# A matmul with a decayed running sum: a quarter of w loaded in eight pieces, the first 32 slots replanned, the last blocks copied in two pieces and stored by two queues

## The chip, the cores and the metric

The kernel runs on one core of a Trainium2 chip. The metric is the device time of one execution in microseconds (us). The kernel before takes 905.96 us, the median of three runs (905.82 to 906.7). The profile belongs to one execution; its span, from the first to the last instruction, is 903.9 us.

## The reference

`x` has shape (16, 2048, 1024), `w` (1024, 1024), `decay` (1024,), all float32. For every batch the product is taken and then summed along time with a decay that each column has for itself:

```python
xw = x @ w
out[:, 0, :] = xw[:, 0, :]
for t in range(1, S):
    out[:, t, :] = decay[None, :] * out[:, t - 1, :] + xw[:, t, :]
```

## The kernel before

**The layout.** Time is cut into 64 chunks of 512 steps (`TL`), two chunks make a group. The 1024 output columns are eight sets `n` of 128 (`K = 8`; the sets 0 to 3 are the first half `h = 0` of the columns, 4 to 7 the second, `R = 4`), and the 1024 input columns are eight sets `k`. TensorE forms 128 columns x 512 or 1024 steps in PSUM with `wsb[:, k, n]` as the weights and a transposed chunk of x, and VectorE runs the scan along time. A pair of a group and a set `n` is a slot. 

**x comes in** through GpSimd's DMA queue, four transfers for a chunk (the quads `q`), converted to bf16 on the way. VectorE transposes it (`T`, or `E` in quarters of a half chunk), and ScalarE or VectorE puts it in order for TensorE (`X`, `Y`, or `F`, `G`). For some products TensorE reads the transposed chunk `xw` directly.

```python
    def load(c, q, j0=0, j1=NJ):
        b, t0 = chunks[c]
        if c not in xb_of:
            xb_of[c] = ring(sb, "xb", 3, [128, NJ, CQ], BF16)
        pin(nc.gpsimd.dma_start(
            out=xb_of[c][quad(q), j0:j1],
            in_=_ap(x, [[D, P], [P * D, j1 - j0], [1, CQ]],
                    (b * S + t0 + j0 * P) * D + q * CQ)))
```

**w comes in** in four quarters: `(h, e)` is the half of the output columns and the parity of `k`. Quarter (0, 0) comes as float32 through the queues of SyncE (SP) and ScalarE (ACT), the other three through GpSimd's, as bf16. `settle` copies one set of 128 rows, `k = 2 m + e`, to its place in `wsb`; it reads all four quads of the staging tile.

```python
    def load_w(queues, h, e):
        for i, q in enumerate((0, 2, 1, 3)):
            pin(queues[i % len(queues)].dma_start(
                out=stage[h, e][quad(q)].rearrange("p (m d) -> p m d", m=M),
                in_=_ap(w, [[2 * D, P], [2 * P * D, M], [1, CH]],
                        (q * CQ + e) * D + h * CH)))

    def settle(h, e, m, copy):
        src = stage[h, e][:, m * CH:(m + 1) * CH]
        pin(copy(out=wcols[:, 2 * m + e, h],
                 in_=src.rearrange("p (q r i) -> p q r i", q=NQ, r=R)))

```

In the plan `U0`, `U1`, `U2` are the quarters (0, 1), (1, 0), (1, 1), and `W` or `w` with a number i is `settle(i // 8, i // 4 % 2, i % 4)` on VectorE or on ScalarE: 0 to 3 settle the first quarter, 4 to 7 the second, 8 to 11 the third, 12 to 15 the fourth. `M0` to `M3` are the half chunks of the first two chunks of x.

**The order of the products at the start**, in which all even k of the first chunk come first, then the odd k, then the second chunk:

```python
        if step == 0:
            heads = [ring(psp, "ps", 3, [128, T]) for _ in range(3)]
            firsts = [ps[:, 0:TL] for ps in heads] + [spares[0]]
            seconds = [ps[:, TL:T] for ps in heads] + [spares[1]]
            for j0, j1 in halves:
                for k in range(0, K, 2):
                    for i in range(R):
                        matmul(firsts[i], i, k, xt_of[0], j0 * P, j1 * P, pairs=xw_of[0])
            for k in range(1, K, 2):
                for i in range(R):
                    matmul(firsts[i], i, k, xt_of[0])
            for k0 in range(0, K, 2):
                for i in range(R):
                    for k in (k0, k0 + 1):
                        matmul(seconds[i], i, k, xt_of[1], 0, H * P,
                               pairs=xw_of[1] if k0 < 4 else None)
            for i in range(R):
                for k in range(K):
                    matmul(seconds[i], i, k, xt_of[1], H * P, TL, H * P,
                           pairs=xw_of[1] if i < 2 else None)
```

**A slot is finished in one of two ways.** An unpaired tile is scanned by VectorE straight from PSUM. A paired one is halved first: ScalarE copies it out (`p`) and scales its odd steps (`g`), GpSimd adds neighbours (`j`), VectorE scans half the steps (`S`), ScalarE (`h`) and GpSimd (`c`) fill in the other half. `flips` names the slots that are turned from one way to the other. `B` is VectorE's transpose of the result into an output tile `ot`; when four of them are there, four stores of 32 rows each go out, and the tile's buffer is one of four.

```python
        def scan(self):
            T, n, so = self.T, self.n, self.so
            if self.paired:
                pin(nc.vector.tensor_tensor_scan(
                    out=so[:, 3:T + 2:2],
                    data0=squares[-1][:, n:n + 1].to_broadcast([128, T // 2]),
                    data1=self.xs[:, 1:T:2],
                    initial=0.0 if self.prev is None else self.prev,
                    op0=ALU.mult,
                    op1=ALU.add,
                ))
            else:
                parts = self.ps if isinstance(self.ps, tuple) else (self.ps,)
                size = T // len(parts)
                for i, ps in enumerate(parts):
                    self.run(ps, i * size, size)

    ...

        def store(self, b, t0):
            n0 = self.ns[0]
            c0 = n0 % R * P
            size = len(self.ns) * P
            for i, q in enumerate((0, 2, 1, 3)):
                pin(self.queues[i % len(self.queues)].dma_start(
                    out=_ap(out, [[D, P], [P * D, self.nj], [1, size]],
                            (b * S + t0 + self.t0) * D + n0 // R * CH + q * CR + c0),
                    in_=self.ot[quad(q), :, c0:c0 + size]))
```

**The plan** says for each slot what is recorded after its products; a capital or small letter is a deed of the kind above, `L` is one transfer of x, `k` keeps the last column for the next group. The first lines, slot -99 being what stands before all products:

```python
-99: "M0 M1 U0 M2 M3 U1 U2 w0 W1 w2 W3 K0 K1 K2 K3 E0 E1 G0 E2 G1 E3 F2 G3 E4 E5 G4 E6 G5 E7 F6 G7 W4 w5 W6 W7 D E8 E9 G8 E10 G9 E11 F10 G11 E12 L E13 G12 L E14 G13 E15 L F14 G15",
0: "p0 z0 W8 W9 W10 W11",
1: "g0",
2: "L S1 L",
3: "p2 z2 L g2 j0 S3 w12 w13 L w14 L w15 k1",
4: "j2 B1 d k3",
5: "p4 L S0 L g4 S2 L k0 h0 j4 B3 h2",
6: "k2 c0 T2 c2 p5 g5 B0 L X2 L",
7: "B2 L L Y2 T3 L z4 z5 j5 p6 S4 z6 L g6 L X3 S5 j6 S7 Y3 L S6 h4 k7 k5 c4 k4 h5 B7",
    ...
flips = (1, 13, 15, -19, -18, -16, -11, -8, -6, -3, -2)
```

**The end.** The last chunk's second half of columns isn't transposed by VectorE but by TensorE, against an identity, in four blocks of 128 steps; each block is copied out of PSUM and stored:

```python
    def ending(i):
        b, t0 = chunks[-1]
        nb = TL // 128
        pts = [ring(psp, name, count, [128, R, 128])
               for name, count in (("spare1", 1), ("ps", 3), ("ps", 3), ("spare", 1))]
        wides = [ring(sb, *spot, [128, NQ, R, P])
                 for spot in (("xb", 3), ("xb", 3), ("xb", 3), ("h", 4))]

        def cross(blocks, rs):
            for i in blocks:
                for r in rs:
                    t = 2 + i * 128
                    pin(nc.tensor.transpose(
                        out=pts[i][:, r], in_=tiles[r - R].so[:, t:t + 128], identity=ident))

        def leave(i, copy):
            pin(copy(out=wides[i].rearrange("p q r i -> p r q i"),
                     in_=pts[i].rearrange("p r (q i) -> p r q i", q=NQ)))
            pin(nc.sync.dma_start(
                out=_ap(out, [[D, 128], [1, CH]], (b * S + t0 + i * 128) * D + CH),
                in_=wides[i].rearrange("p q r i -> p (q r i)")))

        cross((0,), range(R))
        cross((1,), range(R))
        cross((2, 3), range(R - 1))
        cross((2, 3), (R - 1,))
        for i in range(nb):
            leave(i, (nc.scalar.copy, nc.vector.tensor_copy)[i % 2])
```

Every transfer has a semaphore to count to when it lands. GpSimd's transfers share eight of them in turn, those of SP and ACT another eight; a transfer waits until the one that had the semaphore before it has landed. The queue, the engine and the semaphore's place in the turn come from the framework's scheduler, not from the lines above.

Of the kernel before, what the change touches and what calls it, by code (L numbers as in the profile page):

```python
# [14 lines left out]
def _ap(ap_obj: bass.AP, new_ap, extra_offset=0):  # L15
    return dataclasses.replace(
        ap_obj,
        ap=[list(p) for p in new_ap],
        offset=ap_obj.offset + extra_offset,
    )  # L20
# [5 lines left out]
def kernel(  # L26
# [26 lines left out]
    nc = tc.nc  # L53
    pin = tc.keep_in_program_order
    B, S, D = x.shape
    assert w.shape == (D, D)

    NQ = 4
    P = 32
    CQ = D // NQ  # L60
    K = CQ // P
    M = K // 2
# [3 lines left out]
    R = K // 2  # L66
    CH = D // 2
# [8 lines left out]
    def ring(pool, name, count, shape, dtype=FP32):  # L76
        i = turns[name] = turns.get(name, -1) + 1
        return pool.tile(shape, dtype, name=f"{name}{i % count}")

    def quad(q):  # L80
        return slice(q * P, (q + 1) * P)
# [59 lines left out]
    class Tile:  # L141
# [39 lines left out]
        def copy(self):  # L181
            self.xs = sb.tile([128, 2 * TL], FP32, name=f"xs{self.lot % 3}")[:, 0:self.T]
            pin(nc.scalar.copy(out=self.xs, in_=self.ps))  # L183
# [82 lines left out]
    class Outlet:  # L266
# [7 lines left out]
        def store(self, b, t0):  # L274
# [3 lines left out]
            for i, q in enumerate((0, 2, 1, 3)):  # L278
# [9 lines left out]
    stage = {(0, 0): room[0][:, 0:size],  # L288
             (0, 1): room[0][:, size:size * 3 // 2].bitcast(BF16),
             (1, 0): room[1][:, 0:size // 2].bitcast(BF16),  # L290
             (1, 1): room[1][:, size // 2:size].bitcast(BF16)}

    def load_w(queues, h, e):
        for i, q in enumerate((0, 2, 1, 3)):
            pin(queues[i % len(queues)].dma_start(  # L295
                out=stage[h, e][quad(q)].rearrange("p (m d) -> p m d", m=M),
                in_=_ap(w, [[2 * D, P], [2 * P * D, M], [1, CH]],
                        (q * CQ + e) * D + h * CH)))

    def settle(h, e, m, copy):  # L300
        src = stage[h, e][:, m * CH:(m + 1) * CH]
# [5 lines left out]
    rows = const.tile([128, 2, P], FP32, name="rows")  # L307
    touch = const.tile([128, 1], BF16, name="touch")
    load_w((nc.sync, nc.scalar), 0, 0)
    pin(nc.vector.memset(idle, 0.0))  # L310
    pin(nc.vector.memset(rows, 0.0))
# [13 lines left out]
    for q in range(NQ):  # L325
        pin(nc.sync.dma_start(
            out=rows[q * P:q * P + R],
            in_=_ap(decay, [[P, R], [CH, 2], [1, P]], q * CR)))
# [8 lines left out]
        spin(3 if q < NQ - 1 else 2, gates[q])  # L337

    def load_part(i):
        load_w((nc.gpsimd,), *((0, 1), (1, 0), (1, 1))[i])  # L340

    def part_one(i, copy):
        part(i // 8, copy, i % 4, i % 4 + 1, *halves[i // 4 % 2])
# [27 lines left out]
# [12 lines that stand above are left out]
                    pin(nc.tensor.transpose(  # L383
                        out=pts[i][:, r], in_=tiles[r - R].so[:, t:t + 128], identity=ident))

        def leave(i, copy):
            pin(copy(out=wides[i].rearrange("p q r i -> p r q i"),
                     in_=pts[i].rearrange("p r (q i) -> p r q i", q=NQ)))
            pin(nc.sync.dma_start(
                out=_ap(out, [[D, 128], [1, CH]], (b * S + t0 + i * 128) * D + CH),  # L390
                in_=wides[i].rearrange("p q r i -> p (q r i)")))

        cross((0,), range(R))
        cross((1,), range(R))
        cross((2, 3), range(R - 1))
        cross((2, 3), (R - 1,))
        for i in range(nb):
            leave(i, (nc.scalar.copy, nc.vector.tensor_copy)[i % 2])

    slots = [(g, n) for g in groups[:-1] for n in range(K)]  # L400
    slots += [([c], n) for c in groups[-1] for n in range(K)]
# [2 lines left out]
    def turn_and_load(c):  # L404
# [16 lines left out]
        "w": lambda i: settle_one(i, nc.scalar.copy),  # L421
        "M": load_half,
        "U": load_part,
        "E": lambda i: turn(i // 8, *halves[i // 4 % 2], i % 4, i % 4 + 1),
        "F": lambda i: part_one(i, nc.vector.tensor_copy),
# [3 lines left out]
        "d": square_again,  # L429
        "I": identity,  # L430
        "V": ending,
        "p": lambda s: tiles[s % len(slots)].copy(),
        "g": lambda s: tiles[s % len(slots)].odd(),
# [7 lines left out]
        "L": lambda i: load(*loads.pop(0)) if loads else None,  # L441
    }
    agenda = {
        -99: "M0 M1 U0 M2 M3 U1 U2 w0 W1 w2 W3 K0 K1 K2 K3 E0 E1 G0 E2 G1 E3 F2 G3 E4 E5 G4 E6 G5 E7 F6 G7 W4 w5 W6 W7 D E8 E9 G8 E10 G9 E11 F10 G11 E12 L E13 G12 L E14 G13 E15 L F14 G15",
        0: "p0 z0 W8 W9 W10 W11",
        1: "g0",
        2: "L S1 L",
        3: "p2 z2 L g2 j0 S3 w12 w13 L w14 L w15 k1",
        4: "j2 B1 d k3",
        5: "p4 L S0 L g4 S2 L k0 h0 j4 B3 h2",  # L450
        6: "k2 c0 T2 c2 p5 g5 B0 L X2 L",
        7: "B2 L L Y2 T3 L z4 z5 j5 p6 S4 z6 L g6 L X3 S5 j6 S7 Y3 L S6 h4 k7 k5 c4 k4 h5 B7",
        8: "",
        9: "k6 h6 c5 B4",
        10: "p8 g8 c6 T4 z8 p9 j8 g9 B5 X4",
        11: "L j9 B6 p10 S8 L z9 z10 g10 S9 h8",
        12: "j10 Y4 S11 L c8 h9 T5 c9",
        13: "p12 L g12 B9 j12 X5 S10 L",
        14: "Y5 B8 L B11 h10 z12 c10 S13",
        15: "p14 L g14 S12 j14 T6 h12 L",  # L460
        16: "p15 c12 g15 B10 L X6 j15 B12",
        17: "z14 Y6 S14 L B13 z15 h14 S15 p16 z16 c14",
        18: "g16 T7 L h15 j16 p17 g17 B14 z17 c15 X7",
        19: "S16 j17 p18 B15 L g18 L S17 k16 h16 z18 j18",
        20: "Y7 S19 L c16 k17 h17 T8 k19 L c17",
        21: "p20 g20 L S18 X8 j20 B17 B19",
        22: "L h18 p21 c18 B16 k18 g21 B18 Y8 z20 L j21 S20",
        23: "p22 z21 z22 S21 L h20 g22 T9 c20 h21",
        24: "k21 k20 j22 S23 X9 L c21 Y9 B20 L",
        25: "B23 k23 p24 B21 g24 z24 j24 S22 z25",  # L470
        26: "p25 T10 k22 h22 g25 c22 S24 X10 j25",
        27: "B22 p26 S25 g26 z26 Y10 j26",
        28: "S27 h25 h24 c25 S26 c24",
        29: "B27 h26 c26 T11 p28 g28 j28 B24",
        30: "p29 B25 g29 z28 j29 S28 z29 S29",
        31: "h28 p30 c28 B26 g30 h29 B28 j30 z30",
        32: "c29 S31 S30 h30 B29 c30 p32 g32 z32 j32 B30 B31 L L",
        33: "p33 g33 z33 j33 S32 h32 c32 k32 L L",
        -20: "z-20",
        -19: "p-20 g-20",  # L480
# [16 lines left out]
        -2: "S-3 S-4",  # L497
        -1: "S-2 h-4 c-4 a-1 b-1 V",
    }
    flips = (1, 13, 15, -19, -18, -16, -11, -8, -6, -3, -2)  # L500
    later = {}
    begun = {"T": 12, "X": 11, "Y": 11}
    for c in range(5, nch):
# [130 lines left out]
```

## Time and profile before

| what | value |
| --- | --- |
| device time, median of 3 | 905.96 us (905.82 to 906.7) |
| span of the profile | 903.9 us |
| x, through GpSimd's queue | 248 transfers, 256 KB each in SBUF, and 16 of half that |
| w, through GpSimd's queue | 12 transfers, 128 KB each in SBUF, 5.1 us from issue to landing |
| output, through SP's queue | 260 transfers of tiles and four blocks |
| granted TensorE clock | 1.00 |
| moved by DMA | 204.77 MB, mean 227 GB/s |

The page gives for each engine its busy time, the share of the span and the number of instructions; PE is TensorE, DVE VectorE, ACT ScalarE, POOL GpSimd, SP SyncE. The map of 40 slices has a digit for each fortieth of the span, in tenths of busy time. A row of waits names who waited for whom, then the total, the number of times and the longest. A row of the timeline has the start, the time it took, the engine, the line of the kernel, the operation, what it writes and reads, and how often it stands there in a row; in brackets is the idle time of the engine just before, and what ended it. Engine names with a q are queues that only send transfers: their time is the time to send, not the time to land.

### The profile page before, as it was taken

The numbers are of one execution on the slowest core, as the hardware profiler recorded it, in microseconds if no ns is written. First come the engines' busy times: TensorE is split into PE (matmuls) and PEld (weight loads), VectorE is DVE, ScalarE is ACT, GpSimd is POOL, SyncE is SP. The second block draws the span as 40 slices with busy tenths as digits, with TensorE's granted clock in tenths as the row PEclk, the third lists the DMA queues.
The fourth block names the chain that finished last, engine by engine and source line by source line (L and its number), as shares of the span: only waits on it lengthen the run. The fifth ranks groups of instructions, "written<-read, shape, count | busy, mean of one in ns | idle before, by whom it ended". The sixth has DMA issues, their size and how long they took to land.

```text
span 903.9 us, 11988 instructions
## 1 busy us (share of the span) xinstructions
PE 892.7 (99%) x4119; PEld 411.2 (45%) x4201; DVE 826.0 (91%) x628; ACT 684.5 (76%) x951; POOL 655.2 (72%) x753
## 2 busy tenths in 40 slices
PE   9999999999999999999999999999999999999997
PEld 5444444444444444444444444444444444444444
DVE  4999999999999999999998999999999999999997
ACT  4889867777877877877778778778777787787742
POOL 7888678777767768677677677787777776776622
PEclk9999999999999999999999999999999999999999
DMA  9999999999999999999999999999999999999868
GB/s 191 196 215 218 230 213 213 215 239 255 247 242 258 242 257 251 240 242 248 227 235 229 222 234 228 229 229 225 232 228 225 235 230 223 228 231 210 175 144 233
DMA packets 402542, 204.77 MB, mean 227 GB/s; under 512 B 8752, under 2 KB 401456, under 8 KB 402480
## 3 DMA queue, kind: packets, MB, share of 16 engines
q1 hardware_dynamic: 265168, 134.76, 61.3%
q0 software_dynamic: 137024, 68.70, 56.5%
q8 instruction: 33, 0.54, 0.2%
q10 hardware_dynamic: 288, 0.52, 0.2%
q14 instruction: 29, 0.24, 0.1%
HBM read 138.42 MB, written 134.22 MB: 302 GB/s over the span
## 4 chain that ended last, share of the span: by engine, by line
PE 92%; DVE 2%; issue 2%; DMA 1%; POOL 1%; ACT 1%; DVEq 0%; POOLq 0%
PE ps L131 91%; DVE so L221 1%; DMA xb<-in_x_dram 1%; DMA ot<-in_w_dram 1%; PE spare L131 1%; POOL xb L105 1%; ACT xt L123 0%; POOL ot L295 0%; DVE so L201 0%; ACT xs L183 0%; DVE ot L258 0%; DVE xw L115 0%; ACT h L169 0%; POOL xs L196 0%; PE spare L383 0%
## 5 line engine op out<-in xcount | busy, mean ns | idle before, releaser
L131 PE MATMUL ps<-xt,wsb 128*128 128x512 bf16 x3942 | 863.7, 378 | 5.0 <-ACT h L169 0.3
L131 PEld LDWEIGHTS <-wsb 128*128 128x128 bf16 x4152 | 405.9, 98 | 480.3 <-issue 1.2
L196 POOL TENSOR_TENSOR xs<-h,xs 128x512 f32<-128x512 f32 (+1 forms) x189 | 242.0, 1280 | 191.0 <-ACT h L169 84.2
L183 ACT COPY xs<-ps 128x1024 f32<-128x1024 f32 (+1 forms) x189 | 188.7, 998 | 155.3 <-PE ps L131 145.0
L258 DVE STREAM_TRANSPOSE ot<-so 128x1024 f32<-128x1024 f32 (+1 forms) x260 | 300.0, 1191 | 2.8 <-POOL so L190 1.8
L246 POOL TENSOR_TENSOR so<-h,xs 128x512 f32<-128x512 f32 (+1 forms) x189 | 240.5, 1274 | 43.4 <-ACT h L169 27.8
L123 ACT COPY xt<-xw 128x2048 bf16<-128x2048 bf16 (+1 forms) x136 | 242.3, 1790 | 7.8 <-DVE xw L115 7.8
L105 POOL DMA_DIRECT2D xb<-in_x_dram x264 | 174.0, 660 | 3.0 <-DMA ot<-in_w_dram 1.1
L169 ACT ACTIVATE h<-so,dec 128x512 f32<-128x512 f32 (+1 forms) x189 | 144.9, 767 | 26.7 <-DVE so L201 23.6
L115 DVE STREAM_TRANSPOSE xw<-xb 128x2048 f32<-128x2048 f32 (+1 forms) x78 | 147.3, 1901 | 5.9 <-DMA xb<-in_x_dram 5.9
L201 DVE TENSOR_TENSOR_SCAN so<-spare,keep,xs 128x512 f32<-128x512 f32 (+1 forms) x96 | 119.3, 1245 | 27.6 <-POOL xs L196 27.3
L201 DVE TENSOR_TENSOR_SCAN so<-spare,xs 128x512 f32<-128x512 f32 x93 | 113.2, 1219 | 26.8 <-POOL xs L196 23.9
L169 ACT ACTIVATE h<-ps,dec 128x512 f32<-128x512 f32 (+1 forms) x189 | 129.5, 685 | 0.0
L221 DVE TENSOR_TENSOR_SCAN so<-dec,ps 128x1024 f32<-128x1024 f32 x34 | 76.8, 2259 | 1.0 <-ACT h L169 1.0
L221 DVE TENSOR_TENSOR_SCAN so<-dec,keep,ps 128x1024 f32<-128x1024 f32 (+1 forms) x36 | 77.2, 2145 | 0.2
L250 ACT COPY keep<-so 128x1 f32<-128x1 f32 x136 | 25.4, 189 | 13.1 <-DVE so L221 12.6
L192 ACT COPY so<-keep 128x1 f32<-128x1 f32 x96 | 18.3, 191 | 2.0 <-DVE ot L258 1.8
L131 PE MATMUL ps<-xw,wsb 128*128 128x256 bf16 (+1 forms) x68 | 11.2, 301 | 0.1
L190 POOL MEMSET so<- 128x1 f32 x93 | 10.7, 117 | 0.6 <-DVE ot L258 0.6
L131 PE MATMUL spare<-xt,wsb 128*128 128x512 bf16 (+1 forms) x48 | 10.0, 335 | 0.0
L295 POOL DMA_DIRECT2D ot<-in_w_dram x12 | 6.5, 544 | 3.5 <-DMA xb<-in_x_dram 2.4
L320 PE MATMUL spare<-idle 128*128 128x512 bf16 x22 | 7.1, 498 | 1.2 <-DVE idle L310 1.2
(37 smaller groups left out, 36.4 us busy)
## 6 DMA issues: line engine op xcount, KB each, us to landing
out_dram<-ot SPq DMA_DIRECT2D x248, 512.0 KB, 11.0
xb<-in_x_dram POOLq DMA_DIRECT2D x248, 256.0 KB, 7.9
out_dram<-ot SPq DMA_DIRECT2D x12, 256.0 KB, 4.3
xb<-in_x_dram POOLq DMA_DIRECT2D x16, 128.0 KB, 5.8
ot<-in_w_dram POOLq DMA_DIRECT2D x12, 128.0 KB, 5.1
out_dram<-xb SPq DMA_DIRECT2D x3, 256.0 KB
ot<-in_w_dram ACTq DMA_DIRECT2D x2, 256.0 KB, 5.0
ot<-in_w_dram SPq DMA_DIRECT2D x2, 256.0 KB, 4.7
```

What stands on the lines that cost most here:

```text
L105: pin(nc.gpsimd.dma_start(out=xb_of[c][quad(q), j0:j1], in_=_ap(x, [[D, P], [P * D, j1 - j0], [1, CQ]], (b * S + t0 + j0 * P) * D + q * CQ)))
L115: pin(nc.vector.transpose(out=dst.rearrange("p (m j i) -> p j m i", m=M, i=P)[:, j0:j1, m0:m1], in_=src.rearrange("p (j m c) -> p j m c", ...
L123: pin(copy(out=xt_of[c][:, m0:m1, :, j0 * P:j1 * P], in_=src))
L131: pin(nc.tensor.matmul(out=ps[:, t0:t1] if ps.shape[1] >= t1 else ps, lhsT=lhs, rhs=rhs, start=(k == 0 and t0 == start), stop=(k == K - 1),))
L169: pin(nc.scalar.activation(out=h, in_=src, func=mybir.ActivationFunctionType.Copy, scale=dec[:, self.n:self.n + 1]))
L183: pin(nc.scalar.copy(out=self.xs, in_=self.ps))
L196: pin(nc.gpsimd.tensor_tensor(out=odds, in0=self.g, in1=odds, op=ALU.add))
L201: pin(nc.vector.tensor_tensor_scan(out=so[:, 3:T + 2:2], data0=squares[-1][:, n:n + 1].to_broadcast([128, T // 2]), data1=self.xs[:, 1:T:2 ...
L221: pin(nc.vector.tensor_tensor_scan(out=so[:, t + 2:t + 2 + size], data0=dec[:, n:n + 1].to_broadcast([128, size]), data1=ps, initial=befor ...
L246: pin(nc.gpsimd.tensor_tensor(out=self.so[:, 2:T + 2:2], in0=self.h, in1=self.xs[:, 0:T:2], op=ALU.add))
L250: pin(nc.scalar.copy(out=self.keep, in_=self.so[:, self.T + 1:self.T + 2]))
L258: pin(nc.vector.transpose(out=outlet.ot[:, :, c0:c0 + P], in_=self.so[:, 2 + t0:2 + t0 + nj * P].rearrange("p (i t) -> p i t", t=P)))
```

## The change

There are three parts. The second quarter of w, `(0, 1)`, comes in eight transfers instead of four: first the sets m = 0 and 1 of all four quads, then m = 2 and 3, so that the first sets can be settled while the others are on the way. The first 32 slots are planned anew for that: the order of the deeds, which engine settles a set of w, and which slots are paired. At the end, the copies of the last two blocks (2 and 3) are made in two pieces, the three transposes that are early and then the last one, and block 2 is stored by ACT's queue instead of SP's, so that two queues send the last stores.

```diff
--- before.py
+++ after.py
@@ -290,12 +290,12 @@
              (1, 0): room[1][:, 0:size // 2].bitcast(BF16),
              (1, 1): room[1][:, size // 2:size].bitcast(BF16)}
 
-    def load_w(queues, h, e):
+    def load_w(queues, h, e, m0=0, m1=M):
         for i, q in enumerate((0, 2, 1, 3)):
             pin(queues[i % len(queues)].dma_start(
-                out=stage[h, e][quad(q)].rearrange("p (m d) -> p m d", m=M),
-                in_=_ap(w, [[2 * D, P], [2 * P * D, M], [1, CH]],
-                        (q * CQ + e) * D + h * CH)))
+                out=stage[h, e][quad(q)].rearrange("p (m d) -> p m d", m=M)[:, m0:m1],
+                in_=_ap(w, [[2 * D, P], [2 * P * D, m1 - m0], [1, CH]],
+                        (q * CQ + e + m0 * 2 * P) * D + h * CH)))
 
     def settle(h, e, m, copy):
         src = stage[h, e][:, m * CH:(m + 1) * CH]
@@ -337,7 +337,7 @@
         spin(3 if q < NQ - 1 else 2, gates[q])
 
     def load_part(i):
-        load_w((nc.gpsimd,), *((0, 1), (1, 0), (1, 1))[i])
+        load_w((nc.gpsimd,), *((0, 1, 0, 2), (0, 1, 2, M), (1, 0), (1, 1))[i])
 
     def part_one(i, copy):
         part(i // 8, copy, i % 4, i % 4 + 1, *halves[i // 4 % 2])
@@ -383,10 +383,11 @@
                     pin(nc.tensor.transpose(
                         out=pts[i][:, r], in_=tiles[r - R].so[:, t:t + 128], identity=ident))
 
-        def leave(i, copy):
-            pin(copy(out=wides[i].rearrange("p q r i -> p r q i"),
-                     in_=pts[i].rearrange("p r (q i) -> p r q i", q=NQ)))
-            pin(nc.sync.dma_start(
+        def leave(i, copy, queue, pieces):
+            for r0, r1 in pieces:
+                pin(copy(out=wides[i].rearrange("p q r i -> p r q i")[:, r0:r1],
+                         in_=pts[i][:, r0:r1].rearrange("p r (q i) -> p r q i", q=NQ)))
+            pin(queue.dma_start(
                 out=_ap(out, [[D, 128], [1, CH]], (b * S + t0 + i * 128) * D + CH),
                 in_=wides[i].rearrange("p q r i -> p (q r i)")))
 
@@ -395,7 +396,9 @@
         cross((2, 3), range(R - 1))
         cross((2, 3), (R - 1,))
         for i in range(nb):
-            leave(i, (nc.scalar.copy, nc.vector.tensor_copy)[i % 2])
+            leave(i, (nc.scalar.copy, nc.vector.tensor_copy)[i % 2],
+                  nc.scalar if i == 2 else nc.sync,
+                  ((0, R),) if i < 2 else ((0, R - 1), (R - 1, R)))
 
     slots = [(g, n) for g in groups[:-1] for n in range(K)]
     slots += [([c], n) for c in groups[-1] for n in range(K)]
@@ -441,40 +444,40 @@
         "L": lambda i: load(*loads.pop(0)) if loads else None,
     }
     agenda = {
-        -99: "M0 M1 U0 M2 M3 U1 U2 w0 W1 w2 W3 K0 K1 K2 K3 E0 E1 G0 E2 G1 E3 F2 G3 E4 E5 G4 E6 G5 E7 F6 G7 W4 w5 W6 W7 D E8 E9 G8 E10 G9 E11 F10 G11 E12 L E13 G12 L E14 G13 E15 L F14 G15",
-        0: "p0 z0 W8 W9 W10 W11",
-        1: "g0",
-        2: "L S1 L",
-        3: "p2 z2 L g2 j0 S3 w12 w13 L w14 L w15 k1",
-        4: "j2 B1 d k3",
-        5: "p4 L S0 L g4 S2 L k0 h0 j4 B3 h2",
-        6: "k2 c0 T2 c2 p5 g5 B0 L X2 L",
-        7: "B2 L L Y2 T3 L z4 z5 j5 p6 S4 z6 L g6 L X3 S5 j6 S7 Y3 L S6 h4 k7 k5 c4 k4 h5 B7",
+        -99: "M0 M1 U0 U1 M2 M3 U2 U3 w0 W1 w2 W3 K0 K1 K2 K3 E0 E1 G0 E2 G1 E3 F2 G3 E4 E5 G4 E6 G5 E7 F6 G7 W4 W5 W6 w7 D E8 E9 G8 E10 G9 E11 F10 G11 E12 E13 G12 E14 G13 E15 F14 G15",
+        0: "",
+        1: "L S0 L",
+        2: "p1 L",
+        3: "w9 L W8 p2 W11 z1 L W10 B0 z2 g1 L w12 L S3 w13 j1 w14 w15",
+        4: "L g2 k0 L",
+        5: "B3 d k3 p4 j2 S1 g4 L S2 h1 j4 k1",
+        6: "h2 c1 T2 k2 z4 c2 p5 S4 g5 L X2",
+        7: "L B2 j5 B1 Y2 L T3 z5 L k4 L p6 z6 L g6 S5 L h4 j6 X3 S7 c4 k5 h5 L S6 Y3 c5 B4",
         8: "",
... (slots 9 to 31: replanned too)
-        32: "c29 S31 S30 h30 B29 c30 p32 g32 z32 j32 B30 B31 L L",
... (slots 9 to 31: replanned too)
+        32: "c29 S30 S31 B29 h30 c30 p32 g32 z32 j32 B30 B31 L L",
         33: "p33 g33 z33 j33 S32 h32 c32 k32 L L",
         -20: "z-20",
         -19: "p-20 g-20",
@@ -497,7 +500,7 @@
         -2: "S-3 S-4",
         -1: "S-2 h-4 c-4 a-1 b-1 V",
     }
-    flips = (1, 13, 15, -19, -18, -16, -11, -8, -6, -3, -2)
+    flips = (0, 15, 18, 19, 20, 26, 27, -19, -18, -16, -11, -8, -6, -3, -2)
     later = {}
     begun = {"T": 12, "X": 11, "Y": 11}
     for c in range(5, nch):
```

## The prediction

> **What bounds the kernel now.** I read the page's first and second parts first: is one engine full, and all the way through?
>
> ```profile
> span 903.9 us, 11988 instructions
> PE 892.7 (99%) x4119; PEld 411.2 (45%) x4201; DVE 826.0 (91%) x628; ACT 684.5 (76%) x951; POOL 655.2 (72%) x753
> PE   9999999999999999999999999999999999999997
> ```
>
> PE is full in every slice but the last. A busy row can hide waits, so the check is the rate: the chain of waits shows pieces of 49 matmuls of 512 columns, 10.79 us apart with a record or so missing in each (50 x 0.2158 = 10.79). All 4096 such units make 884 us; the first stands at 10.80 us, the last ends at about 896.8. So there are three places where time can be had: before 10.8 us, less than 2 us of waits in the middle, and 7.1 us after the last matmul. All that PE waits for once it multiplies is in the waits of PE, three rows and 0.7 us:
>
> ```profile
> PE ps L131 <- ACT h L169: 0.3, 1, 0.3
> PE ps L131 <- DVE wsb L302: 0.2, 1, 0.2
> PE ps L131 <- DVE so L221: 0.2, 1, 0.2
> ```
>
> The timeline of the first 24 us says what the second of them is:
>
> ```profile
> 8.05 0.55 POOL L295 DMA_DIRECT2D ot<-in_w_dram  x1 [2.04 <-DMA xb<-in_x_dram]
> 10.59 4.92 POOL L105 DMA_DIRECT2D xb<-in_x_dram  x8
> 14.67 0.70 DVE L302 COPY wsb<-ot 128x512 bf16<-128x512 bf16 x3 [0.61 <-DMA ot<-in_w_dram]
> 15.02 0.82 PE L131 MATMUL ps<-xt,wsb 128*128 128x512 bf16 x2 [0.22 <-DVE wsb L302]
> 17.42 1.42 DVE L115 STREAM_TRANSPOSE xw<-xb 128x256 f32<-128x256 f32 x4 [1.49 <-DMA xb<-in_x_dram]
> 18.48 0.84 PE L131 MATMUL ps<-xw,wsb 128*128 128x256 bf16 x6
> ```
>
> PE starts the first odd k at 15.02 instead of 14.64 (the matmul before stands at 14.53 and takes 0.11): 0.38 us lost to w's second quarter, which lands at 14.55. That is what the first part of the change is after. But line 17.42 shows a neighbour with little room: the next half chunk of x lands just before 17.42, its first transpose ends about 17.8, and PE takes it at 18.48.
>
> The end, from the timeline of the last 28 us (the queue of SP and the last copies):
>
> ```profile
> 875.81 20.87 SPq L279 DMA_DIRECT2D out_dram<-ot  x14
> 897.74 0.59 ACT L387 COPY xb<-spare 128x512 f32<-128x512 f32 x1 [1.67 <-PE spare L383]
> 898.35 1.62 SPq L389 DMA_DIRECT2D out_dram<-xb  x3
> 898.94 0.58 ACT L387 COPY xb<-ps 128x512 f32<-128x512 f32 x1 [0.61 <-PE ps L383]
> 899.05 0.69 DVE L387 COPY h<-spare 128x512 f32<-128x512 f32 x1 [0.18 <-PE spare L383]
> 900.07 0.40 SPq L389 DMA_DIRECT2D out_dram<-h  x1
> ```
>
> SP sends stores without a break up to 896.7 and then the four blocks. Transfers, not copies, end the kernel: the table by stages gives 262 GB/s at 0.99 of the DMA engines for 888 to 891 us, and 376 GB/s at 1.00 for 900 to 902.
>
> [...] with one sender the engines already stand at 1.00 in 900 to 902. [...] the first w transfer on POOL stands at 8.05, just after the x transfer that used its semaphore landed at 7.77. So a sender in a wait holds back all it has to send later. [...]
>
> **Part 1, w's second quarter in eight transfers.** Same bytes, half as much each (64 rows of 1 KB instead of 128). GpSimd has eight semaphores for its transfers and takes them in turn, so transfer i waits for transfer i-8 to have landed. Before, the four w transfers and the next four of x went out at 8.05, 8.99, 9.53, 10.06, 10.59, 11.23, 11.88, 12.49. Now all eight of these places go to w, and x's third half chunk starts at about 13.05 instead of 10.59: **2.46 us later**. Before, the DMA queue was never empty (193 GB/s from 8 to 20 us); its backlog cannot cover 2.5 us. From issue to the first byte I take 2.7 us: the shortest in this stretch is 2.83, the shortest after an idle gap anywhere in the trace 2.65.
> - Gain: the first four pieces (m = 0, 1) are sent by 10.06, so land by about 13.7. W4 and W5 are done before 14.64, and the 0.38 us go. The last piece leaves at 12.49, has its bytes at 15.2 and lands at about 16.1; W6 is ready at 16.5, needed at 16.4.
> - Loss: x's half chunk has its first byte at 13.05 + 2.7 = 15.75, four transfers at 0.68 us each (their spacing before) make 18.5, landing 0.6 later: 19.1 instead of 17.3. Transpose 0.4, so PE can go on at about 19.7 instead of 18.48: **+1.2 us** against before. [...]
>
> **Part 2, the plan of the first 32 slots.** Nine unpaired scans before, nine now; so the sums per engine stay. On the path: S0 (2.27 us on DVE) now stands before W8, so W8 ends about when step 4 needs it; on ACT, copy 1, w9, copy 2 and odd 1 (1.0 + 0.55 + 1.0 + 0.7) stand before w12 to w15 (0.54 each), which come 0.1 to 0.5 us late for the odd k of step 4. Against this the wait at 41.59 us (0.25) should go, since T2 no longer stands behind B2's neighbours. Net about zero, and every stall in this stretch stays in the end time because PE has no reserve later. Both parts: **+1.0 us** (from 0 to +1.8).
>
> **Part 3, the last two blocks.** Two things in the instruction lists of the built program matter.
> - The two-piece copies: in both, the first piece waits for the last transpose of its block (PE counts 4200 and 4201), the second for nothing. So nothing starts earlier, and ACT needs 0.48 + 0.27 - 0.1 overlap = 0.65 us instead of 0.58 (from 0.59 for 512 and 1.0 for 1024 columns).
> - ACT's store took a place in the turn of the eight semaphores shared by SP and ACT, and the scheduler gave it a place among stores that leave at about 886, long before its own end:
>
> ```
> SP   store of ot1, first row set     waits HW5 >= 512, adds 16 to HW5
> ACT  store of block 2 (its last)     waits HW6 >= 496, adds 16 to HW6
> SP   store of ot1, second row set    waits HW6 >= 512, adds 16 to HW6
> SP   two more of ot1, four of ot2, blocks 0, 1 and 3
> ```
>
> 512 on HW6 is reached only when block 2, the work of the last matmuls, has landed. Before, that count was reached by a store of some us earlier. So SP stands still from about 888.5, and behind it wait seven stores of 262,144 bytes and three blocks of the same size. Step by step, without the shift of part 1: ACT's copies end at 898.94 + 0.65 = 899.6, its store goes at 899.65 and lands about 2.6 later (as block 0: issue 898.35, landed 900.98), 902.25; SP sends at 902.3, bytes flow 0.9 later, 903.2; seven stores are 1.835 MB at 0.260 MB/us = 7.06; three blocks 0.786 MB at 0.376 = 2.09; bytes end at 912.35. Before they ended at about 902.7 and the span at 903.9, so 1.2 more: 913.55. That is **+9.65 us**.
>
> **Sum.** 905.96 + 9.65 + 1.0 = 916.6.
>
> **Rivals.** (a) SP does not stand still, or the order of landing is kinder than the list says: then only parts 1 and 2 count, and the earlier second sender is worth nothing as the engines are full: 905.5 to 907.5. For it speaks that the author meant an earlier end; against it the count on HW6. I give it 7 in 100. (b) x's third half chunk is not late, since a 64-row transfer might reach the engines sooner: then the 0.38 and 0.25 us are gained and the end is about 915.0. (c) The eight small pieces starve the queue further and w's third quarter also comes late, 1 us more: 917.6. (d) The idle DMA time before 899 lets the late stores run at the rate of the blocks (376 instead of 260): 7.06 becomes 4.9, the end is 914.4. Against it, the same stores at a share of 0.99 give 262.
>
> **Range and chances.** The size of part 3 is uncertain by about 1 us (rate, latency), parts 1 and 2 by about 1 us: 914.4 to 918.4. Slower by over 2% would need 924, which nothing here reaches; faster by over 2% is impossible with PE at 99%. Within 2% it is, but on the slow side.
>
> **What would show it.** In the profile after: SP's queue waits about 12 to 14 us near 888 to 902, then sends eight or more transfers in a row; PE's last matmul within 2 us of 896.8; the DMA share near 0 about 893 to 899 and near 1 after 903; a wait of PE at about 18.5 us for xw, and none at 14.64; the ACT copies of the end in two pieces back to back, no earlier than before. If the span is near 904, rival (a) holds and my reading of HW6 is wrong.

## The result and the profile after

The changed kernel takes **918.47 us** (median of 6 runs, 917.76 to 922.65) against 905.85 for the kernel before beside it (905.45 to 906.7): a ratio of 1.015, with an interval of 1.0128 to 1.0172. That is 12.6 us slower, within 2% but far outside what the measurement is uncertain by. The prediction was 916.6 with 914.4 to 918.4, so the result lies 0.07 us above its range. The profiled run took 918.07 us and its span is 916.3 us, 12.4 more than before.

The page of the changed kernel, first and second part:

```profile
span 916.3 us, 11994 instructions
PE 892.3 (97%) x4119; PEld 410.7 (45%) x4201; DVE 825.2 (90%) x628; ACT 684.1 (75%) x954; POOL 657.1 (72%) x756
PE   8999999999999999999999999999999999999993
DMA  9999999999999999999999999999999999999674
```

PE's work is the same within 0.4 us; so the added time is standing still. It shows at both ends: the first slice of PE fell from 9 to 8, and the last three slices of the DMA row read 6, 7 and 4, where the kernel before has 8, 6 and 8. Those two ends are read in turn.

The waits of SP's queue in the changed kernel (total us, times, longest):

```profile
SPq L279 <- DVE ot L258: 266.2, 47, 35.8
...
SPq L279 <- DMA out_dram<-xb: 13.2, 1, 13.2
```

The first row is the usual one, a store waiting for a finished tile, and costs nothing. The second is new: one single wait of 13.2 us, for a *store of a block* (`out_dram<-xb`), by a store of another tile. No data connects the two; what they share is a semaphore, as the prediction's list of the built program says and the trace confirms: the released store adds to the one that ACT's store added to. The timeline of the last 33 us shows what the wait does (start, duration, engine, operation, count, and in brackets the idle time ahead of it):

```profile
882.46 27.48 SPq L279 DMA_DIRECT2D out_dram<-ot  x12
...
900.60 0.65 ACT L388 COPY xb<-ps 128x384 f32<-128x384 f32 x2 [0.62 <-PE ps L383]
...
901.27 0.38 ACTq L390 DMA_DIRECT2D out_dram<-xb  x1
910.04 2.08 SPq L390 DMA_DIRECT2D out_dram<-xb  x2
912.23 0.40 SPq L390 DMA_DIRECT2D out_dram<-h  x1
```

A row's duration runs from the first to the last of its instructions, so the 27.48 us of the first row contain the hold. Narrowed to 900 us and later, the same queue begins with the instruction that was released:

```profile
903.35 6.59 SPq L279 DMA_DIRECT2D out_dram<-ot  x7
```

ACT sends block 2 at 901.27 and it lands at 903.25; SP is released at 903.35 and only then sends the seven tile stores that were ready long before, and after them three blocks. The table by stages (stretch, length, busy time of PE, PEld, DVE, ACT and POOL, clock, DMA share, GB/s) shows both halves of it:

```profile
893.00:901.00 8.00, 7.67 (x50) 4.85 (x48) 7.56 (x11) 2.48 (x6) 1.47 (x2) 1.00 0.01 2
905.00:911.00 6.00, 0.00 (x0) 0.00 (x0) 0.00 (x0) 0.00 (x0) 0.00 (x0) 0.52 1.00 244
```

For eight microseconds PE works while the DMA engines do nothing (0.01); then they do everything alone (1.00).

The 244 GB/s are a mean of two rates. The first 1.6 us after the hold are slow and the stretch behind them is not:

```profile
904.20:905.80 1.60, 0.00 (x0) 0.00 (x0) 0.00 (x0) 0.00 (x0) 0.00 (x0) 0.82 0.92 162
905.80:911.00 5.20, 0.00 (x0) 0.00 (x0) 0.00 (x0) 0.00 (x0) 0.00 (x0) 0.50 1.02 258
```

The kernel before has the same start when its stores begin again near 894.4 us, with PE busy:

```profile
894.40:896.00 1.60, 1.60 (x13) 1.14 (x12) 1.60 (x3) 0.46 (x1) 0.00 (x0) 1.00 0.95 167
896.00:898.00 2.00, 2.00 (x18) 1.56 (x17) 1.90 (x3) 0.33 (x2) 0.73 (x1) 1.00 1.05 263
```

At the other end, the first microseconds of the changed kernel's timeline:

```profile
8.95 3.92 POOL L295 DMA_DIRECT2D ot<-in_w_dram  x7 [0.41 <-DMA xb<-in_x_dram]
12.86 4.60 POOL L105 DMA_DIRECT2D xb<-in_x_dram  x8
14.50 0.81 PE L131 MATMUL ps<-xt,wsb 128*128 128x512 bf16 x2
19.45 1.42 DVE L115 STREAM_TRANSPOSE xw<-xb 128x256 f32<-128x256 f32 x4 [2.92 <-DMA xb<-in_x_dram]
19.95 0.84 PE L131 MATMUL ps<-xw,wsb 128*128 128x256 bf16 x6 [1.84 <-DVE xw L115]
```

The first odd k starts at 14.50 without a wait, as the change wanted. But x's half chunk is sent at 12.86 instead of 10.59, is transposed from 19.45 instead of 17.42, and PE stands still for 1.84 us before 19.95. PE's last product of the scan starts at 898.35 instead of 896.70: 1.66 us of the 12.4 are made here, and the rest at the end.

### The profile page after: what moved, and what is told of

Read it like the earlier page. It is cut to its first block, busy times and chain, and to the rows that moved or that the text cites. A ratio compares the mean times of both kernels' runs of the same rounds, so it can differ in the third digit from the quotient of the medians.

```text
span 916.3 us, 11994 instructions
## 1 busy us (share of the span) xinstructions
PE 892.3 (97%) x4119; PEld 410.7 (45%) x4201; DVE 825.2 (90%) x628; ACT 684.1 (75%) x954; POOL 657.1 (72%) x756
## 4 chain that ended last, share of the span: by engine, by line
PE 95%; DMA 2%; POOL 1%; issue 1%; ACT 0%; DVE 0%; DVEq 0%; ACTq 0%; POOLq 0%
PE ps L131 94%; DMA xb<-in_x_dram 1%; PE spare L131 1%; DMA ot<-in_w_dram 1%; POOL ot L295 0%; POOL xb L105 0%; PE spare L383 0%; PE ps L383 0%; ACT wsb L302 0%; DVE h L388 0%; DVEq L632 0%; ACTq L302 0%; POOLq L621 0%
## 5 line engine op out<-in xcount | busy, mean ns | idle before, releaser
L221 DVE TENSOR_TENSOR_SCAN so<-dec,ps 128x1024 f32<-128x1024 f32 x35 | 79.1, 2260 | 0.7 <-ACT h L169 0.6
L221 DVE TENSOR_TENSOR_SCAN so<-dec,keep,ps 128x1024 f32<-128x1024 f32 (+1 forms) x35 | 74.8, 2137 | 0.1
L131 PE MATMUL ps<-xw,wsb 128*128 128x256 bf16 (+1 forms) x68 | 11.2, 301 | 1.8 <-DVE xw L115 1.8
L295 POOL DMA_DIRECT2D ot<-in_w_dram x16 | 8.7, 550 | 4.1 <-DMA xb<-in_x_dram 3.7
```

What stands on the lines that cost most here:

```text
L131: pin(nc.tensor.matmul(out=ps[:, t0:t1] if ps.shape[1] >= t1 else ps, lhsT=lhs, rhs=rhs, start=(k == 0 and t0 == start), stop=(k == K - 1),))
L221: pin(nc.vector.tensor_tensor_scan(out=so[:, t + 2:t + 2 + size], data0=dec[:, n:n + 1].to_broadcast([128, size]), data1=ps, initial=befor ...
```

## The experiments

**Theory A**: the hold of SP through the shared semaphore makes about 10 us; ACT's sending alone costs nothing. **Theory B**: the eight transfers, not the new plan, make the rest, as they put x back (from split_only on, the expectations call it theory A1). Rivals: the two-piece copies or the second queue cost something by themselves; the new plan is what loses; a small number of large pieces of w would have helped. Each run stands beside runs of the kernel before, whose median was 905.91, 906.0 or 906.1; the ratios and differences below are to that.

### Only the place in the turn: turn_late

The kernel after, with one ordering edge for the scheduler, so that ACT's store takes its semaphore after SP's store of block 1. Each engine runs the same instructions in the same order; only the semaphores change hands.

```diff
-            pin(queue.dma_start(
+            sent = pin(queue.dma_start(
...
+            if queue is nc.scalar:
+                tc.add_manual_dep(sent.ins, stores[-1].ins.name, ...NoSync..., reason="turn")
+            stores.append(sent)
```

> The changed kernel, with one edge more for the scheduler: ACT's store of block 2 may only be placed after SP's store of block 1. The instructions on every engine are the same; ACT's store takes its semaphore 45 stores' places later, behind all stores of the output tiles. Theory A (SP was held by the count on HW6, which only block 2 could complete): the hold of 13.2 us goes, and only the later end of TensorE (898.35 instead of 896.70 us) remains: 907.2 to 907.9 us. Rival B (a second queue or the two-piece copies slow the last stores by themselves): stays above 914 us.

Measured: 909.62 us (907.68 to 910.2, 5 runs), ratio 1.0036 (1.0023 to 1.0049). The profiled run is the one of 907.68. In its timeline the queues of SP and ACT from 890 us on read:

```profile
889.90 8.53 SPq L279 DMA_DIRECT2D out_dram<-ot  x8
900.14 1.11 SPq L392 DMA_DIRECT2D out_dram<-xb  x2
901.40 0.37 ACTq L392 DMA_DIRECT2D out_dram<-xb  x1
901.62 0.33 SPq L392 DMA_DIRECT2D out_dram<-h  x1
```

ACT sends at the same moment as in the kernel after (901.40 and 901.27), yet SP's tile stores are out by 898.4 and its blocks follow. Nothing but the turn of the semaphores differs, so the hold is that turn. By the order of the stores in the two traces, ACT's store moved back by 16 places, not the 45 of the expectation. The median is 1.7 us above the range expected: the two runs at a mean clock of 0.999 took 907.68 and 908.66 us, the other three, at 0.997 or 0.998, took 909.62 to 910.2. The 25-run comparison below takes this up.

### The new end alone, and without the hold: tail_only and tail_turn_late

tail_only is the kernel before with the change's end; tail_turn_late adds the edge of turn_late to it.

```diff
 # tail_only, against the kernel before
-            leave(i, (nc.scalar.copy, nc.vector.tensor_copy)[i % 2])
+            leave(i, (nc.scalar.copy, nc.vector.tensor_copy)[i % 2],
+                  nc.scalar if i == 2 else nc.sync,
+                  ((0, R),) if i < 2 else ((0, R - 1), (R - 1, R)))
```

> The kernel before with the new end alone (two-piece copies, block 2 stored by ACT); w in four transfers, the old plan. Theory A: SP is held again, for about 11.5 us, TensorE ends as before: 916.0 to 917.5 us. Rival C (the shift of the first 50 us collides with something later and is what costs the time): under 907 us.

> The kernel before with the new end alone and ACT's store placed behind SP's store of block 1 for the scheduler. This is what the end was meant to be, without the hold. The DMA engines are full from 899.25 us on, and the first of the two pieces starts no earlier than the whole copy did: 905.8 to 906.3 us, no gain that can be measured. If two senders or two pieces are worth something, 905.3 to 905.7 us.

Measured: tail_only 917.09 us (4 runs, ratio 1.0124, 1.011 to 1.0137), tail_turn_late 906.2 (13 runs, ratio 1.0002, 0.9994 to 1.001). The waits of SP's queue in tail_only repeat the hold to the tenth:

```profile
SPq L279 <- DMA out_dram<-xb: 13.2, 1, 13.2
```

So **the hold costs 917.09 - 906.2 = 10.9 us**, and without it no gain of pieces with a second sender can be measured. tail_turn_late's timeline shows why: ACT's two pieces still start after PE's last transpose, and take 0.65 us instead of 0.58.

```profile
899.15 0.65 ACT L390 COPY xb<-ps 128x384 f32<-128x384 f32 x2 [0.61 <-PE ps L383]
899.83 0.37 ACTq L392 DMA_DIRECT2D out_dram<-xb  x1
```

From 900 to 902 us the DMA engines are at a share of 1.00 with 374 GB/s, against 1.00 with 376 before; two senders find the same full engines.

### The new front alone: all_sp and front_only

all_sp is the kernel after with block 2 sent by SP, pieces kept. front_only is the kernel after with the whole old end.

```diff
 # all_sp, against the kernel after
-                  nc.scalar if i == 2 else nc.sync,
+                  nc.sync,
```

> The changed kernel with block 2 stored by SP; the copies stay in two pieces. Theory A: no hold, 907.2 to 907.9 us, the same as with the late turn within 0.3 us, since the DMA engines were full at the end and a second sender is worth nothing. If a second queue is worth something, this is slower than the late turn by 0.2 to 0.5 us.

> The changed kernel with the old end as a whole (copies in one piece, all blocks stored by SP): the eight transfers and the new plan alone. TensorE's last product 1.6 to 1.7 us later than before, the rest as before: 907.3 to 907.8 us. The two-piece copies are worth less than 0.1 us against this either way.

Measured: 907.94 us (11 runs, ratio 1.0028, 1.0019 to 1.0036) and 907.81 (9 runs, ratio 1.0025, 1.0015 to 1.0035). all_sp lies 0.04 us above the range expected. It was also to lie within 0.3 us of turn_late, and the medians are 1.7 us apart; without the runs at the lower mean clock, three in each, all_sp has 907.18 to 908.16 and turn_late its two of 907.68 and 908.66. The new front costs 1.9 us. Front (+1.9) and end (11.2 with the hold) together would make 13.1; the whole change has 12.6.

### Split or plan: split_only and plan_only

split_only is the kernel before with the eight transfers, under the old plan; plan_only has the new plan with the old four transfers, and the old end.

```diff
 # split_only, against the kernel before (load_w also takes m0 and m1, as in the change)
-        load_w((nc.gpsimd,), *((0, 1), (1, 0), (1, 1))[i])
+        load_w((nc.gpsimd,), *((0, 1, 0, 2), (0, 1, 2, M), (1, 0), (1, 1))[i])
...
-        -99: "M0 M1 U0 M2 M3 U1 U2 w0 ...
+        -99: "M0 M1 U0 U1 M2 M3 U2 U3 w0 ...
```

> The kernel before with w's second quarter in eight transfers by row sets and nothing else (old plan, old end). Theory A1 (eight small transfers take the places of the next half chunk of x in the turn of GpSimd's eight semaphores, and x's transfers then leave 2.3 us later): TensorE waits for xw near 18 us for about 1.5 us, last product about 1.2 us later than before, 906.9 to 907.6 us. Rival A2 (the loss of the new front comes from the new plan): this one is as before or 0.3 us faster, under 906.1 us.

> The kernel before with the new plan of the first 32 slots and nothing else (w's second quarter in four transfers by quads, old end). Theory A1 (the new plan alone costs little, the loss comes from the late x): the wait for wsb near 14.6 us as before, w12 to w15 late by 0.1 to 0.5 us, the wait near 41.6 us gone: 905.6 to 906.4 us. Rival A2 (the new plan carries the loss): over 907 us.

Measured: split_only 908.79 us (6 runs, ratio 1.003, 1.0018 to 1.0041), plan_only 906.28 (13 runs, ratio 1.0002, 0.9994 to 1.001). So the plan by itself makes no difference that can be measured, and the split alone costs more than the whole front: theory B. But split_only was expected at 906.9 to 907.6. A part of the reason stands in PE's timeline of it:

```profile
18.10 0.38 PE L131 MATMUL spare<-xt,wsb 128*128 128x512 bf16 x1
20.83 1.44 PE L131 MATMUL ps<-xw,wsb 128*128 128x256 bf16 x6 [2.35 <-DVE xw L115]
```

PE waits 2.35 us for x, where about 1.5 were expected, and then six matmuls take 1.44 us that take 0.84 in the kernels before and after. The table by stages says the same in the clock's column (the sixth figure after the length, counting each engine's busy time as one):

```profile
18.00:20.80 2.80, 0.48 (x3) 0.10 (x1) 0.47 (x2) 0.00 (x0) 1.72 (x4) 0.99 1.26 151
20.80:24.10 3.30, 3.27 (x16) 2.23 (x16) 2.04 (x7) 1.96 (x4) 2.40 (x5) 0.50 1.26 190
```

After the wait of 2.35 us TensorE ran at half its clock: 0.50 in the mean of the 3.30 us from 20.80 to 24.10, and 0.99 in the 2.80 us before and the 3.90 us behind. At half speed that stretch loses half of its length; by these figures my estimate is **1.65 us on top of the wait**. The clock is only part of the miss: three of the six runs have the lower mean clock of 0.997 and took 908.98 to 909.77 us, but the other three, at 0.999 or 1.000, still took 907.9 to 908.6.

### Is it the clock: front_fill and after_fill

If the long runs of the new front come from the clock falling in PE's wait near 18 us, products that nobody uses, put into that wait, should take them away. Both kernels below compute the same output and seven 512-column products more.

```diff
+            for _ in range(7):
+                pin(nc.tensor.matmul(out=seconds[R - 1], lhsT=gates[0], rhs=idle, start=True, stop=True))
```

> The eight transfers and the new plan with the old end, and seven products of 512 columns that nothing uses, put where TensorE waits for the second chunk (into PSUM that the next product starts anew). They fill 1.5 us of the wait of 1.7 us. Theory D (some runs of the new front are 2 us longer because TensorE's clock falls after this wait: mean clock 0.997 there against 0.999): all runs within 1 us of each other, 907.4 to 908.3 us. Rival E (the longer runs have another cause): some runs stay near 909.5 us.

> The changed kernel as a whole, with seven products that nothing uses in TensorE's wait near 18 us. Of the changed kernel's six times two are 3.5 us over the others, with a mean clock of 0.991 against 0.994. Theory D (TensorE's clock falls to half for some us after the wait): no such time here, all within 1.2 us of each other, median 917.5 to 918.5 us. Rival E (they come from the late stores at the end): some times near 921 us or more stay.

Measured: front_fill 908.27 us (907.22 to 908.76, 13 runs; the spread of 1.54 us is more than the 1 us expected), after_fill 918.49 (918.11 to 918.97, 4 runs, ratio 1.0138, 1.0122 to 1.0153). In the table by stages of after_fill PE is full, where it was nearly empty in split_only, and the clock stays:

```profile
18.00:20.80 2.80, 2.80 (x20) 1.76 (x19) 1.73 (x5) 1.29 (x3) 2.24 (x5) 1.00 1.19 150
20.80:24.10 3.30, 3.30 (x29) 2.58 (x27) 1.34 (x4) 1.24 (x3) 1.93 (x4) 1.00 1.26 187
```

Of the 25 runs of turn_late, all_sp and front_only, 8 took 909.4 us or more, at a mean clock of 0.997 or 0.998; of the 13 filled runs none did. Of the 6 runs of the kernel after two took over 921 us at a clock of 0.991 (the others 0.993 or 0.994); of the 4 filled ones none passed 919. So the long runs of the new front go with a lower clock, and with the wait filled there were none. For the kernel after, two of six against none of four is too few to show it, and no trace of one of its long runs was kept. The fill is no gain all the same: the median of front_fill is 0.5 us *above* front_only's 907.81; in the profiles PE goes on at 20.34 instead of 20.18. Not settled is why only some runs lose the clock. In the kernel after, the wait of 1.84 us was followed by a clock of 1.00 from 20 to 24 us, in the profiled runs of turn_late, all_sp and front_only the clock is 1.00 over the first 25 us with waits of 1.3 to 1.8 us, and in split_only it is 0.50 after 2.35 us. But none of those four profiled runs is one of the long ones, so what sets the long runs apart was not shown.

### Whole row sets instead: sets_old_plan and sets_new_plan

In the kernel after x was sent 2.27 us later than before (12.86 instead of 10.59) and its half chunk landed 2.04 us later (19.33 instead of 17.29), so the four places more in GpSimd's queue, and in its turn of eight semaphores, are enough to explain the delay: in both traces every transfer of this queue from the ninth on starts only when the one eight places ahead of it has landed (268 of 268 before, 272 of 272 after). If that is all, four transfers that each bring one row set m of all four quads (128 rows of 1 KB) should give the gain without the loss.

```diff
+    def load_w_sets(h, e):
+        for m in range(M):
+            pin(nc.gpsimd.dma_start(
+                out=stage[h, e][:, m * CH:(m + 1) * CH],
+                in_=_ap(w, [[CQ * D, NQ], [2 * D, P], [1, CH]], (e + m * 2 * P) * D + h * CH)))
```

> The kernel before with w's second quarter in four transfers as before, but each of them one row set m of all four quads (128 rows of 1 KB) instead of all row sets of one quad: so the first set can be settled early and no further place in the turn of semaphores is taken. Theory A1: the wait of 0.2 to 0.9 us for wsb near 14.6 us goes, no wait for xw near 18 us comes: 905.2 to 905.6 us, faster than before by 0.3 to 0.6 us. Rival A2 (any earlier start of the odd k only moves the wait to the next half chunk of x): as before within 0.2 us.

> As the one with four transfers by row sets, but with the new plan of the first 32 slots (old end). Theory A1: x and w's third and fourth quarters come at the old times, so the new plan's wait for w12 is small: 905.0 to 905.8 us. If the new plan is by itself worse (ACT's order puts w12 to w15 late), it is slower than the old plan with row sets by 0.2 to 0.5 us.

Measured: 908.59 us (9 runs, ratio 1.0026, 1.0016 to 1.0036) and 908.99 (5 runs, ratio 1.0033, 1.002 to 1.0045). Both missed by 3 us, on the wrong side. In sets_old_plan the four landed at 14.54, 14.76, 15.87 and 16.87 us; of the old four the *last* landed at 14.55. The waits of PE now have x as their first row, twice:

```profile
PE ps L131 <- DVE xw L115: 2.1, 2, 1.1
```

The stretch of 11 to 14 us moved 140 GB/s; in the kernel before, the same stretch has 194, and its PE is full:

```profile
11.00:14.00 3.00, 2.05 (x19) 1.59 (x18) 1.30 (x5) 1.23 (x3) 2.04 (x4) 1.00 1.24 140
```

The page counts 1,536 more packets under 512 bytes than before (10,288 against 8,752), all of 4 bytes and all in GpSimd's queue: 384 more for each of the four, where every other transfer of this queue has 16. So these two runs don't isolate the places in the queue: x was sent at 10.69 us, at nearly its old place, and was late all the same. That these packets are the cause of the lower rate is likely and not shown; why they are there is open.

## Why the prediction was off, and where it was right

Right, each as "What would show it" had put it: the hold (13.2 us in SP's queue; 12 to 14 said) and its cause, the count on HW6 (turn_late changes that alone); the DMA share of 0.01 up to 901 us and 1.00 after; the two pieces back to back and no earlier, 0.65 us as worked out; no wait at 14.64 and one for xw near 18.5; the last product within 2 us of 896.8. Rival (a) falls with the hold, (b) with x's landing at 19.33, (d) with the stores' rate, 258 GB/s once they ran. Part of (c) came true: w's third quarter landed to 26.25 us instead of 23.77, and w12 made PE wait (below).

So the mechanism was right, and what failed are sizes. The sum of the profile was 903.9 + 9.65 + 1.0 = 914.55 and the span is 916.3. The 1.75 us between them lie in these terms, read from the packets and instructions of the trace:

| term of the sum | predicted | measured | difference |
| --- | --- | --- | --- |
| parts 1 and 2, shift of PE's last product | +1.0 | +1.66 | +0.66 |
| ACT's store from its issue to its landing | 2.6 | 1.98 | -0.6 |
| from the landing of ACT's store to the first byte of SP's | 0.95 | 0.94 | 0.0 |
| seven stores, from the first byte until their 1.835 MB are reached | 7.06 | 7.84 | +0.8 |
| three blocks, from there to the last byte | 2.09 | 3.01 | +0.9 |
| last byte to the end of the span | 1.2 | 1.24 | 0.0 |

The experiments have the same two errors: the new end alone cost 11.2 us where 9.65 stood, the new front alone 1.9 where 1.0 stood. The steps that failed:

- **"seven stores are 1.835 MB at 0.260 MB/us = 7.06; three blocks 0.786 MB at 0.376 = 2.09"**. This is the largest miss: together they took 10.85 us instead of 9.15. Both rates were read in the middle of a stretch in which the DMA engines were full, and were used from the first byte to the last. In the middle they hold (258 GB/s from 905.8 to 911 us, 392 from 913 to 914). But the first 1.6 us ran at 162 GB/s, the microsecond in which the last store and the blocks overlap at 298, and the last 1.1 us at 101. The slow start could be seen in the kernel before: the reading **"SP sends stores without a break up to 896.7"** takes a row of 14 merged transfers for an unbroken one, but SP paused from 891.6 to 893.5 us, and its stores then began at 167 GB/s. Why they begin slowly is open.
- **"PE can go on at about 19.7 instead of 18.48: +1.2 us"**. It went on at 19.95, 1.47 us later than before. x landed at 19.33 with 19.1 said, but that is two errors which nearly cancel, and partly luck. Its first byte came at 14.42, 1.56 us after the sending at 12.86, where 2.7 stood. Its four transfers then landed at 16.48, 17.23, 17.99 and 19.33, up to 1.34 us apart, where 0.68 stood.
- **"Net about zero"** for part 2 agrees with the plan alone (plan_only 1.0002), but not beside late transfers. PE waits 0.4 us for w12, which the prediction had in its list of risks and not in its sum:

```profile
PE ps L131 <- ACT wsb L302: 0.4, 1, 0.4
28.81 2.18 ACT L302 COPY wsb<-ot 128x512 bf16<-128x512 bf16 x4 [0.25 <-DMA ot<-in_w_dram]
```

The risk was put down to the copies that stand before w12 on ACT. In the trace ACT is done with them and waits for w's fourth quarter, which landed at 28.71 instead of 26.00 us; plan_only, with w on time, has no such wait. So it belongs to rival (c).

Missing altogether is that a wait of PE can cost the clock (0.50 after the 2.35 us in split_only). By their mean clock of 0.991 it may have done so in two of the six runs. They move the median from 918.24 (the four others) to 918.47.

## What to carry to other kernels

Before you give a store to a second queue, look at which semaphore it gets and who has it next: a transfer that ends with the last work of the kernel may not stand in the turn ahead of stores that are ready earlier, or it stops a queue it shares no data with (13.2 us here, and one ordering edge removed it). Splitting a transfer to have its first half sooner costs places in the same queue and its turn of semaphores, and what stands behind pays: here x was sent at 12.86 us instead of 10.59, 0.4 us were won on w and 1.8 us of waiting came in for x. A rate read in the middle of a full stretch of stores doesn't hold for its beginning and its end: here 258 GB/s in the middle, 162 in the first 1.6 us and 101 in the last 1.1. Add to a wait of TensorE near 2 us the chance of losing the clock after it: in split_only 2.35 us of waiting were followed by 0.50 over 3.30 us, while 1.84 us in the kernel after cost no clock in its trace.

## What the runs showed of the hardware

- A wait of TensorE of 2.35 us was followed by a clock of 0.50 over the 3.30 us from 20.80 to 24.10 us (split_only). With waits of 1.3 to 1.8 us in the profiled runs of turn_late, all_sp and front_only, 8 of their 25 runs were longer by some 2 us at a lower mean clock, and with the wait filled none of 13 (front_fill).
- Stores in packets of 512 bytes began at 162 GB/s (after the hold) and 167 GB/s (in the kernel before, at 894.4 us) and ran at 258 and 263 behind that, at a DMA share of 0.92 to 1.05. With a nearly full share the rate was not the same.
- With w in eight transfers of 64 rows in the queue's eight places, the DMA engines moved 138 GB/s from 14 to 18 us (the kernel after), and 189 in the same stretch before.
- In sets_old_plan four transfers over 128 rows of 1 KB came with 384 packets of 4 bytes more each, and the last of them landed 2.3 us later (16.87 us) than the last of four over 32 rows of the same total size before (14.55 us).
